# Fetching V rows apart from U rows, after GELU, in one of two gathers of a PEER trunk

## The chip, the cores and the metric

The kernel runs on one core of a Trainium2 chip. The metric is device time in microseconds, the median of several runs; one more execution is recorded by the hardware profiler. The engines are PE (TensorE, matmuls), PEld (its weight loads), DVE (VectorE), ACT (ScalarE), POOL (GpSimd, which issues the indirect DMAs), and SP (SyncE, which issues the plain DMAs). Sixteen DMA engines carry what both issue.

## The reference

A decoder trunk of four layers on 256 tokens of 1024 numbers. Each layer is a token mixer (HGRN2, FoX, Mamba-2 SSD, HGRN2) followed by a PEER feed-forward block. What the change touches is PEER:

```python
s = einsum('mhcd,hckd->mhck', q, sub_keys)         # 8 heads, 2 halves, 128 keys
sv, si = top_k(s, 16)                              # then the best 16 of 16 x 16 sums: idx, gates
u = take(u_tab, idx, axis=0)                       # (tokens, 8, 16, 1024) float32
v = take(v_tab, idx, axis=0)
act = gelu(einsum('md,mhkd->mhk', xb, u), approximate=False) * gates
return einsum('mhk,mhkd->md', act, v)
```

Each token picks 8 x 16 = 128 of a layer's 16384 experts and needs the U row and the V row of each, 4 KB apiece. `xb` is an RMS-normed token times `norm_ffn`; the inputs scale that weight by 7.294 (`factors = {'norm_ffn': 7.294, ...}`), and the rows of `peer_u` are independent normals of deviation 1/32. A V row whose GELU is 0 adds nothing to the sum.

## The kernel before

The work is cut into 8 stages (`STAGES`): layer l, token half t, 128 tokens each. A stage's expert sums run as 64 iterations, 8 heads times 8 pairs of experts (`pairs`, `NQ` = 8), while the mixer, the queries and the routing of the next stage run beside them in small steps.

An iteration i has two gathers, g = 0 and 1. Gather g brings, for 64 tokens and two experts each, 128 rows to 128 partitions (partition = 64 j + token). The table `uv` holds U and V of an expert side by side, so a row is 8 KB. There are eight buffers (`NGB` = 8, in `GB`, parts of the tile `arena`), each [128, 2048] float32: U in columns 0 to 1023, V behind it. Gather n = 2 i + g goes to buffer n % 8.

The order of work in each iteration is written out by hand (`ctx.enter_context(tc.manual_schedule())`); each engine runs its own instructions in that order, and waits are derived from which bytes an instruction reads and writes:

- `fetches(i)` (L1263, called at L1395) issues gathers on POOL's queue up to number 2 i + 7, which is pair i + 3, as far as `route` has their indices. A gather waits for the last reader of its buffer, the matmuls of `spread(i - 1)`.
- `dot(i, 0)` and `dot(i, 1)` (L1269): one DVE instruction each (`scalar_tensor_tensor`) multiplies U with the token rows `XR`, in place, and sums to `dots`.
- `spread(i)` (L1280): ACT takes GELU of both sums in one instruction, multiplies each by its gate, and scales a stack of two 64 x 64 identities to `dg`; PE then adds `dg` times V to the two banks `accs[s][e]`, e = 0 and 1 for the halves of V's columns, eight matmuls of 64 rows in all as the profile counts them (four in the source: two e, two g). The matmuls are at L1296.
- `route_steps` (three steps of the routing of a later head; DVE and some ACT), `others()` (the copies and vector work that follow the last step's matmuls) and `products_()` (the next step's matmuls).

`route` (L1164) ends by writing a head's indices as float32 and gates to `gs` and the int32 indices to `ix` (L1223).

Toward a stage's end: at i % 64 = 62 what is left of the side work is finished, and `repeated()` (L1241) turns the next stage's tokens on PE; at 63, ACT and DVE copy them to `XR` between and after the dots. At the first iteration of the next stage, between `dot(i, 0)` and `dot(i, 1)`, the first step of the side work adds the finished sums to the residual `h` (`normed`, called from `ready` with `accs.pop`, L1335): DVE waits there for the last matmul of the stage before. Weights come by SP's queue, 1 MB a unit (`loads`), three in flight beside those that have a place of their own.

Of the kernel before, what the change touches and what calls it, by code (L numbers as in the profile page):

```python
# [10 lines left out]
F32 = mybir.dt.float32  # L11
BF16 = mybir.dt.bfloat16
I32 = mybir.dt.int32
U32 = mybir.dt.uint32
U8 = mybir.dt.uint8
AF = mybir.ActivationFunctionType
OP = mybir.AluOpType
AX = mybir.AxisListType

P = 128  # L20
T = 256
D = 1024
DC = D // P
DEPTH = 4
# [4 lines left out]
NQ = TOPK // 2  # L29
NGB = 8  # L30
NRAW = 3
STAGES = 2 * DEPTH

KIND = ("hg", "fox", "ssd", "hg")
# [131 lines left out]
def trunk(ctx: ExitStack, tc: tile.TileContext, d: dict, out: bass.AP):  # L166
    nc = tc.nc
# [3 lines left out]
    wk2 = ctx.enter_context(tc.tile_pool(name="wk2", bufs=2))  # L171
# [22 lines left out]
    GB = [at_["gb"][:, i * 2 * D:(i + 1) * 2 * D] for i in range(NGB)]  # L194
# [12 lines left out]
    vec = Vector()  # L207
# [5 lines left out]
    def act(o, i, f, **k):  # L213

        if f not in ghosts:
            table[0] = f
        nc.scalar.activation(o, i, f, **k)  # L217
# [15 lines left out]
    m64 = cpool.tile([P, 64], F32, name="m64")  # L233
# [46 lines left out]
    def bank():  # L280
        return psp.tile([P, 512], F32, name="ps")
# [882 lines left out]
    def route(s, hh):  # L1164

        l = s // 2
        sv = wk2.tile([P, 2, TOPK], F32, name="sv")
        si = wk2.tile([P, 2, TOPK], U32, name="si", bufs=1)
        sf = wk2.tile([P, 2, TOPK], F32, name="sf", bufs=1)
        ts = wk2.tile([P, TOPK], F32, name="ts")  # L1170
        ti = wk2.tile([P, TOPK], U32, name="ti", bufs=1)
        ab = wk2.tile([P, 2, TOPK], U32, name="ab", bufs=1)
        af = wk2.tile([P, 2, TOPK], F32, name="af", bufs=1)
        cs = wk2.tile([P, TOPK * TOPK], F32, name="cs", bufs=1)
        eq = cs.bitcast(BF16).rearrange("p (c k j) -> p c k j", c=2, k=TOPK)
        cs = cs.rearrange("p (a b) -> p a b", a=TOPK)
        ix = wk2.tile([P, 2, NQ], I32, name="ix", bufs=4)
        gs = wk2.tile([P, 2, 2, NQ], F32, name="gs", bufs=4)
        gt = wk2.tile([P, 4], F32, name="gt")
        ig = wk2.tile([P, 2, TOPK], F32, name="ig")  # L1180
        yield from top16([(sv[:, c], si[:, c], SS[:, hh, c]) for c in range(2)])
        vec.tensor_copy(sf, si)
        tm(cs, sv[:, 0].unsqueeze(2).to_broadcast([P, TOPK, TOPK]),
           sv[:, 1][:, None, :].to_broadcast([P, TOPK, TOPK]), op=OP.add)
        yield
        yield from top16([(ts, ti, cs.rearrange("p a b -> p (a b)"))])
        vec.tensor_scalar(ab[:, 0], ti, 4, None, op0=OP.logical_shift_right)
        vec.tensor_scalar(ab[:, 1], ti, 15, None, op0=OP.bitwise_and)
        vec.tensor_copy(af, ab)
        m, z, r = (gt[:, i:i + 1] for i in range(3))  # L1190
        vec.tensor_scalar(m, ts[:, 0:1], -1.0, None, op0=OP.mult)
        act(ig[:, 1], ts, AF.Exp, bias=m, accum_out=z)
        yield
        eqv = eq.rearrange("p c k j -> p (c k) j")
        tm(eqv, C("iota")[:, None, :].to_broadcast([P, 2 * TOPK, TOPK]),
           af.rearrange("p c k -> p (c k)").unsqueeze(2).to_broadcast([P, 2 * TOPK, TOPK]), op=OP.is_equal)
        yield
        tm(eq, eq, sf.unsqueeze(2).to_broadcast([P, 2, TOPK, TOPK]), op=OP.mult)
        yield
        vec.tensor_reduce(af.rearrange("p c k -> p (c k)"), eqv, axis=AX.X, op=OP.add)  # L1200
        vec.tensor_scalar(sf[:, 0], af[:, 0], float(P), float(l * P * P), op0=OP.mult, op1=OP.add)
        tm(ig[:, 0], sf[:, 0], af[:, 1], op=OP.add)
        yield
        igv = ig.rearrange("p c (q j) -> p c q j", j=2)
        places = [(slice(j * 64, j * 64 + 64), g, slice(g * 64, g * 64 + 64), j) for j in range(2) for g in range(2)]

        def scaled():
            vec.reciprocal(r, z)
            vec.tensor_scalar(ig[:, 1], ig[:, 1], r, None, op0=OP.mult)

        if (s, hh) == (0, 0):

            for o, g, i, j in places:
                vec.tensor_copy(ix[o, g], igv[i, 0, :, j])
            scaled()
            for o, g, i, j in places:
                vec.tensor_copy(gs[o, g, 1], igv[i, 1, :, j])
        else:
            scaled()
            yield  # L1220
            for o, g, i, j in places:
                vec.tensor_copy(gs[o, g], igv[i, :, :, j])
            vec.tensor_copy(ix, gs[:, :, 0])  # L1223
        got[s, hh] = ix, gs

    heads = [(s, hh) for s in range(STAGES) for hh in range(8)]
# [28 lines left out]
    accs = {}  # L1255
    sent = [0]

    def fetch(n):
        (s, hh, q), g = pairs[n // 2], n % 2
        nc.gpsimd.indirect_dma_start(GB[n % NGB], None, d["uv"],  # L1260
                                     bass.IndirectOffsetOnAxis(ap=got[s, hh][0][:, g, q:q + 1], axis=0))

    def fetches(n):  # L1263

        while sent[0] < 2 * len(pairs) and sent[0] < 2 * n + NGB and pairs[sent[0] // 2][:2] in got:
            fetch(sent[0])
            sent[0] += 1

    def dot(i, g):  # L1269
        if g == 0:  # L1270
            acts[i] = wk2.tile([P, 3, 2], F32, name="dots", bufs=4)
        u = GB[(2 * i + g) % NGB][:, 0:D]
        stt(u, u, 1.0, XR[:, g], op0=OP.mult, op1=OP.mult, accum_out=acts[i][:, 0, g:g + 1])

    def warm(n, b, x):

        for _ in range(n):
            nc.tensor.matmul(b, x[:, 0:P], x[:, 0:512], start=True, stop=True)

    def spread(i):  # L1280
        s, hh, q = pairs[i]
        a = acts.pop(i)
        dg = wk2.tile([P, 2, 64], F32, name="dg", bufs=4)
        act(a[:, 1], a[:, 0], AF.Gelu)
        for g in range(2):
            act(a[:, 2, g:g + 1], a[:, 1, g:g + 1], AF.Copy, scale=got[s, hh][1][:, g, 1, q:q + 1])
        for g in range(2):
            act(dg[:, g], m64, AF.Copy, scale=a[:, 2, g:g + 1])
        if hh == 0 and q == 0:
            accs[s] = [accp.tile([P, 512], F32, name="acc") for _ in range(2)]  # L1290
        if i == len(pairs) - 1:
            warm(3, bank(), cst)
        for e in range(2):
            for g in range(2):
                v = GB[(2 * i + g) % NGB][:, D + e * 512:D + (e + 1) * 512]
                nc.tensor.matmul(accs[s][e][g * 64:g * 64 + 64], dg[:, g], v, start=hh == 0 and q == 0,  # L1296
                                 stop=hh == 7 and q == NQ - 1)


    mixers = {"hg": hgrn, "fox": fox, "ssd": ssd}  # L1300
# [67 lines left out]

    for s in range(STAGES):
        work = side(s) if s else chain(first, side(0))  # L1370
        state = {"open": False, "done": False, "pe": 0.0, "dve": 0.0, "cost": 0.0, "slot": 0}

        def products_(force=False):

            state["slot"] += 1
            if state["done"] or not (force or state["cost"] < SIDE[s] * state["slot"] / SPAN):
                return
            state["pe"], state["dve"] = pe[0], dve[0]
            r = next(work, work)
            state["done"] = r is work  # L1380
            state["open"] = r is None
            state["pe"] = pe[0] - state["pe"]
            state["dve"] = dve[0] - state["dve"]

        def others():

            if state["open"]:
                d0 = dve[0]
                next(work)
                state["open"] = False  # L1390
                state["cost"] += max(state["pe"] / 4.6, (state["dve"] + dve[0] - d0) / 2.2, 0.5)

        for i in range(64 * s, 64 * s + 64):
            new, end = i % 64 == 0 and s > 0, i % 64 == 63 and s + 1 < STAGES
            fetches(i)  # L1395
            dot(i, 0)
            if end:
                for o, b in x[:2]:
                    nc.scalar.copy(o, b)
            elif new:  # L1400

                products_(True)
                others()
            dot(i, 1)
            spread(i)
            if end:
                (_, b), (o, c) = x[2:]
                nc.scalar.copy(x[2][0], b)
                vec.tensor_copy(o, c)
            route_steps(3, i // 8 + 3)  # L1410
            others()
            products_()
            if i % 64 == 62 and s + 1 < STAGES:
                while not state["done"]:
                    others()
                    products_(True)
                others()
                x = repeated()
            if table[0] is not AF.Gelu:
                act(spare, eps, AF.Gelu)  # L1420
        others()
        for _ in work:
            pass
# [17 lines left out]
```

## Time and profile before

| | |
|---|---|
| median of three runs | 3184.8 us (3184.7 to 3185.98) |
| profiled execution, its own time | 3185.7 us |
| its span, first to last instruction | 3183.9 us |
| mean granted TensorE clock | 0.904 |
| first and last gather issued at | 117.2 and 3157.7 us |
| gathers, of them waited for by DVE | 1024, 540 |
| read from HBM | 1299.92 MB |

How to read it: the span is cut by the gathers. Up to about 120 us the kernel computes the first mixer and the first indices; then 512 iterations run, some 5.9 us each ((3157.7 - 117.2) / 512), and after the last gather there are 26 us to the end of the span. A stretch's row of the busy-time view has its bounds and length, the busy us of PE, PEld, DVE, ACT and POOL with their instruction counts, then the granted clock, the DMA engines' busy share and GB/s. In a row of a group of instructions the numbers behind the count are busy us and mean ns of one, then the idle time just before them and what ended it. In a row of waits they are us in total, times, and the longest.

### The profile page before, as it was taken

The page shows a single profiled execution, that of the slowest core. Times are in us where ns is not written, and L with a number is a line of the kernel's source. Part 1 is how long each engine was busy: PE and PEld are TensorE (multiplying, and loading weights), DVE is VectorE, ACT ScalarE, POOL GpSimd, SP SyncE. Part 2 cuts the span into 40 slices and gives each one's busy share as a digit, 9 for nine tenths or more (in the row PEclk, how much of TensorE's full clock was granted, in tenths as well). Part 3 has the DMA queues.
Part 4 walks back from the last instruction along what each step waited for, and adds up shares of the span by engine and source line. Part 5 has one row for each costly group of instructions (what it writes and reads, how often), then busy time and mean ns, then how long its engine had stood idle before and what let it go on. Part 6 is the DMA issues. An engine that isn't in the chain of part 4 may idle for free.

```text
span 3183.9 us, 30834 instructions
## 1 busy us (share of the span) xinstructions
PE 2470.2 (78%) x8610; PEld 1095.2 (34%) x8610; DVE 2115.5 (66%) x5584; ACT 1351.3 (42%) x3895; POOL 1189.5 (37%) x1032
## 2 busy tenths in 40 slices
PE   9888787877787876889878898778876877865655
PEld 4433333332333423344333443333332333332222
DVE  2576657675676756878567786476666767676764
ACT  3354324353344523577334773244433543333332
POOL 0243334343343424433334333244433433344443
PEclk9999898988899988999989998989988999898787
DMA  7899999999999999999999999999999999999997
GB/s 299 339 420 421 421 421 419 421 407 421 407 420 421 407 422 414 404 421 421 417 417 401 421 419 415 416 403 410 421 421 421 401 421 421 421 414 421 415 417 330
DMA packets 180025, 1303.02 MB, mean 409 GB/s; under 512 B 19984, under 2 KB 20368, under 8 KB 21520
## 3 DMA queue, kind: packets, MB, share of 16 engines
q0 software_dynamic: 147456, 1073.81, 81.8%
q1 hardware_dynamic: 32400, 227.24, 17.3%
q8 instruction: 72, 1.18, 0.2%
q14 instruction: 97, 0.79, 0.1%
HBM read 1299.92 MB, written 1.05 MB: 409 GB/s over the span
## 4 chain that ended last, share of the span: by engine, by line
DMA 58%; PE 14%; DVE 11%; issue 9%; ACT 4%; POOL 3%; POOLq 0%; DVEq 0%; ACTq 0%
DMA arena<-in_uv,ix 58%; DVE arena L204 8%; PE acc L1296 7%; PE pj L239 5%; POOL arena L1260 3%; PE ps L239 2%; ACT dots L217 1%; ACT L217 1%; DVE cs L204 1%; ACT dg L217 1%; PE ps L243 0%; DVE si L204 0%; ACT arena L217 0%; DVE sv L204 0%; DVE af L204 0%
## 5 line engine op out<-in xcount | busy, mean ns | idle before, releaser
L1260 POOL DMA_INDIRECT arena<-in_uv,ix x1024 | 1185.4, 1158 | 1968.6 <-PE acc L1296 1411.0
L204 DVE SCALAR_TENSOR_TENSOR arena<-arena 128x1024 f32<-128x1024 f32 (+3 forms) x1282 | 1322.1, 1048 | 878.5 <-DMA arena<-in_uv,ix 834.9
L1296 PE MATMUL acc<-arena,dg 128*64 128x512 f32 x4096 | 1285.2, 714 | 693.9 <-ACT dg L217 693.2
L1296 PEld LDWEIGHTS acc<-arena,dg 128*64 128x64 f32 x4096 | 466.0, 152 | 1326.4 <-ACT dg L217 1004.2
L217 ACT ACTIVATE dots<-dots 128x2 f32<-128x2 f32 x512 | 103.2, 202 | 1549.4 <-DVE arena L204 1549.3
L239 PE MATMUL pj<-raw,arena 128*128 128x512 f32 (+1 forms) x1368 | 635.5, 607 | 3.8 <-DMA raw<-in_ssm 2.8
L217 ACT ACT_TABLE_LOAD x325 | 417.0, 1283 | 6.8 <-DVE arena L204 0.8
L239 PEld LDWEIGHTS pj<-raw,arena 128*128 128x128 f32 x1368 | 249.8, 193 | 393.6 <-issue 377.4
L217 ACT ACTIVATE dg<-m,dots 128x64 f32<-128x64 f32 x1024 | 292.5, 333 | 0.0
L239 PE MATMUL pj<-arena 128*128 128x512 f32 x568 | 267.4, 616 | 0.3 <-DVE arena L204 0.3
L217 ACT ACTIVATE dots<-dots,gs 128x1 f32<-128x1 f32 x1024 | 245.6, 287 | 16.7
L239 PEld LDWEIGHTS pj<-arena 128*128 128x128 f32 x568 | 106.4, 197 | 162.5 <-issue 153.2
L239 PE MATMUL ps<-arena 128*128 128x128 f32 (+3 forms) x992 | 129.5, 286 | 1.1 <-ACT arena L1125 0.9
L239 PEld LDWEIGHTS ps<-arena 128*128 128x128 f32 (+2 forms) x992 | 102.7, 167 | 65.3 <-issue 39.0
L243 PEld LDWEIGHTS ps<-fst,arena 128*128 128x128 f32 x568 | 67.3, 147 | 85.5 <-issue 39.9
L243 PE MATMUL ps<-fst,arena 128*128 128x128 f32 x568 | 90.9, 288 | 4.5 <-ACT arena L1124 2.5
L217 ACT ACTIVATE arena<-arena 128x512 f32<-128x512 f32 (+3 forms) x132 | 67.7, 555 | 42.0 <-DVE arena L204 39.5
L204 DVE DVE_READ_ACCUMULATOR arena<-arena 128x1 f32 x1024 | 85.0, 83 | 0.0
L204 DVE FIND_INDEX8 si<-sv,arena 128x8 uint32<-128x128 f32 x256 | 69.9, 286 | 0.0
L239 PE MATMUL ps<-cst,arena 128*128 128x128 f32 (+3 forms) x288 | 67.0, 360 | 0.0
L204 DVE MAX8 sv<-arena 128x8 f32<-128x128 f32 x256 | 61.8, 283 | 5.7 <-ACT arena L1129 5.7
L217 ACT ACTIVATE arena<-ps 128x512 f32<-128x512 f32 (+3 forms) x114 | 43.7, 425 | 29.7 <-PE ps L239 29.0
(116 smaller groups left out, 1248.9 us busy)
## 6 DMA issues: line engine op xcount, KB each, us to landing
raw<-in_hg SPq DMA_DIRECT2D x57, 1024.0 KB, 9.4
raw<-in_ssm SPq DMA_DIRECT2D x56, 1024.0 KB, 9.4
raw<-in_wq SPq DMA_DIRECT2D x32, 1024.0 KB, 9.2
raw<-in_fox SPq DMA_DIRECT2D x24, 1024.0 KB, 9.2
arena<-in_wq SPq DMA_DIRECT2D x17, 1024.0 KB, 16.7
arena<-in_uv,ix POOLq DMA_INDIRECT x1024, 14.9
arena<-in_hg SPq DMA_DIRECT2D x15, 1024.0 KB, 14.1
arena<-in_keys SPq DMA_DIRECT2D x4, 1024.0 KB, 9.3
```

What stands on the lines that cost most here:

```text
L204: return getattr(nc.vector, name)(o, *a, **k)
L217: nc.scalar.activation(o, i, f, **k)
L239: nc.tensor.matmul(o, w, m, start=start, stop=stop)
L243: nc.tensor.transpose(o, i, ident)
L1260: nc.gpsimd.indirect_dma_start(GB[n % NGB], None, d["uv"], bass.IndirectOffsetOnAxis(ap=got[s, hh][0][:, g, q:q + 1], axis=0))
L1296: nc.tensor.matmul(accs[s][e][g * 64:g * 64 + 64], dg[:, g], v, start=hh == 0 and q == 0, stop=hh == 7 and q == NQ - 1)
```

## The change

From the ninth iteration on, gather 0 brings its U rows only (from a view `parts` of the table with twice as many rows of half the length, at row 2 x index), into columns 0 to 1023. Its V rows come by a DMA of their own, `second(i)`, issued after `dot(i, 1)` into columns 1024 to 2047, at row 2 x index + 1. Where the GELU of gather 0 is equal to 0, a large number is added to the index, so that it lies beyond the table, and the DMA is told to leave such rows out; the buffer keeps what it held, and that is multiplied by 0. For the last two iterations of a stage (`early`) V is fetched without regard to GELU, one iteration ahead of the dots. GELU is taken for each gather apart, right after its dot. The matmuls of gather 0 move to `spread(i + 2)` (`LAG` = 2), ahead of those of (i + 2, 1); at the end of a stage those of its last two iterations are done in their own iteration as well. Gather 1 is as it was.

```diff
+LAG = 2
+WHOLE = 8
+FAR = 1048576.0
...
             vec.tensor_copy(ix, gs[:, :, 0])
+            vec.tensor_scalar(ix[:, 0], gs[:, 0, 0], 2.0, None, op0=OP.mult)
+            vec.tensor_scalar(gs[:, 0, 0], gs[:, 0, 0], 2.0, 1.0, op0=OP.mult, op1=OP.add)
...
+    parts = d["uv"].rearrange("r (k n) -> (r k) n", k=2)
+
+    def early(i):
+        return i % 64 >= 64 - LAG
+
     def fetch(n):
-        (s, hh, q), g = pairs[n // 2], n % 2
-        nc.gpsimd.indirect_dma_start(GB[n % NGB], None, d["uv"],
+        i, g = divmod(n, 2)
+        s, hh, q = pairs[i]
+        to, src = GB[n % NGB], d["uv"]
+        if not g and i >= WHOLE:
+            to, src = to[:, 0:D], parts
+        nc.gpsimd.indirect_dma_start(to, None, src,
                                      bass.IndirectOffsetOnAxis(ap=got[s, hh][0][:, g, q:q + 1], axis=0))
...
+    def second(i):
+
+        if i < WHOLE or i >= len(pairs):
+            return
+        s, hh, q = pairs[i]
+        iv = wk2.tile([P, 1], I32, name="iv", bufs=4)
+        row = got[s, hh][1][:, 0, 0, q:q + 1]
+        to = GB[2 * i % NGB][:, D:2 * D]
+        if early(i):
+            nc.vector.tensor_copy(iv, row)
+            nc.gpsimd.indirect_dma_start(to, None, parts, bass.IndirectOffsetOnAxis(ap=iv, axis=0))
+        else:
+            far = wk2.tile([P, 1], F32, name="far", bufs=2)
+            nc.vector.tensor_scalar(far, acts[i][:, 1, 0:1], 0.0, FAR, op0=OP.is_equal, op1=OP.mult)
+            nc.vector.tensor_tensor(iv, far, row, op=OP.add)
+            nc.gpsimd.indirect_dma_start(to, None, parts, bass.IndirectOffsetOnAxis(ap=iv, axis=0),
+                                         bounds_check=2 * DEPTH * P * P - 1, oob_is_err=False)
 
     def dot(i, g):
...
+        act(acts[i][:, 1, g:g + 1], acts[i][:, 0, g:g + 1], AF.Gelu)
...
+    diags = {}
 
     def spread(i):
...
-        act(a[:, 1], a[:, 0], AF.Gelu)
...
-            act(dg[:, g], m64, AF.Copy, scale=a[:, 2, g:g + 1])
+            diags[i, g] = wk2.tile([P, 64], F32, name="dg%d" % g, bufs=4 - g)
+            act(diags[i, g], m64, AF.Copy, scale=a[:, 2, g:g + 1])
...
+        sums = [(i, 1)]
+        if i < WHOLE or early(i):
+            sums.append((i, 0))
+        if (i - LAG, 0) in diags:
+            sums.insert(0, (i - LAG, 0))
         for e in range(2):
-            for g in range(2):
-                v = GB[(2 * i + g) % NGB][:, D + e * 512:D + (e + 1) * 512]
-                nc.tensor.matmul(accs[s][e][g * 64:g * 64 + 64], dg[:, g], v, start=hh == 0 and q == 0,
-                                 stop=hh == 7 and q == NQ - 1)
+            for j, g in sums:
+                v = GB[(2 * j + g) % NGB][:, D + e * 512:D + (e + 1) * 512]
+                nc.tensor.matmul(accs[s][e][g * 64:g * 64 + 64], diags[j, g], v, start=j % 64 == 0,
+                                 stop=j % 64 == 63)
...
             fetches(i)
+            if early(i + 1):
+                second(i + 1)
             dot(i, 0)
...
             dot(i, 1)
+            if not early(i):
+                second(i)
             spread(i)
```

More of the change, by code (lines that the diff above doesn't have):

```diff
@@ L1282, in spread @@
         a = acts.pop(i)
-        dg = wk2.tile([P, 2, 64], F32, name="dg", bufs=4)
-        act(a[:, 1], a[:, 0], AF.Gelu)
         for g in range(2):
@@ L1292, in spread @@
             warm(3, bank(), cst)
-        for e in range(2):
-            for g in range(2):
-                v = GB[(2 * i + g) % NGB][:, D + e * 512:D + (e + 1) * 512]
-                nc.tensor.matmul(accs[s][e][g * 64:g * 64 + 64], dg[:, g], v, start=hh == 0 and q == 0,
-                                 stop=hh == 7 and q == NQ - 1)
+        sums = [(i, 1)]
[3 more added lines that the diff above has]
+            sums.insert(0, (i - LAG, 0))
+        for e in range(2):
+            for j, g in sums:
+                v = GB[(2 * j + g) % NGB][:, D + e * 512:D + (e + 1) * 512]
+                nc.tensor.matmul(accs[s][e][g * 64:g * 64 + 64], diags[j, g], v, start=j % 64 == 0,
+                                 stop=j % 64 == 63)
+        for k in sums:
+            diags.pop(k)
     mixers = {"hg": hgrn, "fox": fox, "ssd": ssd}
```

## The prediction

> **What bounds the kernel now.** I read the page's head, slices and queues first, then the chain that ended last, then the waits, and last the busy time by stretches.
>
> ```profile
> span 3183.9 us, 30834 instructions
> ...
> PE 2470.2 (78%) x8610; PEld 1095.2 (34%) x8610; DVE 2115.5 (66%) x5584; ACT 1351.3 (42%) x3895; POOL 1189.5 (37%) x1032
> ...
> GB/s 299 339 420 421 421 421 419 421 407 421 407 420 421 407 422 414 404 421 421 417 417 401 421 419 415 416 403 410 421 421 421 401 421 421 421 414 421 415 417 330
> DMA packets 180025, 1303.02 MB, mean 409 GB/s; under 512 B 19984, under 2 KB 20368, under 8 KB 21520
> ...
> q0 software_dynamic: 147456, 1073.81, 81.8%
> q1 hardware_dynamic: 32400, 227.24, 17.3%
> ...
> DMA 58%; PE 14%; DVE 11%; issue 9%; ACT 4%; POOL 3%; POOLq 0%; DVEq 0%; ACTq 0%
> ...
> L1260 POOL DMA_INDIRECT arena<-in_uv,ix x1024 | 1185.4, 1158 | 1968.6 <-PE acc L1296 1411.0
> ...
> L217 ACT ACTIVATE dots<-dots 128x2 f32<-128x2 f32 x512 | 103.2, 202 | 1549.4 <-DVE arena L204 1549.3
> ...
> arena<-in_uv,ix POOLq DMA_INDIRECT x1024, 14.9
> ```
> ```profile
> POOL arena L1260 <- PE acc L1296: 1411.0, 428, 10.5
> ...
> DVE arena L204 <- DMA arena<-in_uv,ix: 834.9, 540, 5.4
> ```
> ```profile
> 300.00:360.00 60.00, 50.18 (x175) 21.34 (x173) 41.06 (x99) 23.42 (x64) 21.44 (x20) 0.91 1.01 421
> ...
> 1600.00:2000.00 400.00, 336.27 (x1227) 153.92 (x1228) 295.33 (x807) 207.23 (x548) 144.39 (x126) 0.93 1.01 415
> ...
> 3100.00:3184.00 84.00, 47.93 (x126) 17.99 (x126) 40.09 (x68) 21.25 (x83) 26.96 (x23) 0.78 0.81 335
> ```
>
> The last two numbers of a stretch are the DMA engines' busy share and GB/s. From the third slice to the last but one the rate is 401 to 422, and the share is 1.01 even where PE is busiest (336 of 400 us): the 16 DMA engines are full. DVE waits 835 us for gathers, and POOL 1411 us for a buffer that PE must free; these waits are symptoms of the full queue. The two gathers of an iteration carry 82% of the bytes. So a byte not moved is worth its time at 421 GB/s, a packet added costs time, and work on an engine is free until it lets the DMA ring run dry.
>
> **The bytes.** Of 512 iterations, the first 8 (WHOLE) stay as they were and 504 are split. Sixteen of those (two a stage, `early`) bring their V rows unconditionally; 488 bring V after GELU and leave rows out: 128 x 4096 B = 0.524 MB each, 255.9 MB in all. How many GELUs are exactly 0 no trace shows. The dot product of a normed token (its weights scaled by 7.294) with a row of independent normals of variance 1/1024 is normal with deviation 7.294. GELU is x times the normal distribution function. If zero starts where 1+erf rounds away in float32, at -5.4, 23.0% of rows go; if where the product itself leaves float32's normal range, near -13, 3.7%. I take the middle, 13.3%: 34.0 MB, at 421 GB/s **-81 us** (ends -23 and -140). A row out of bounds is taken to cost nothing; the other case is a rival.
>
> **The packets.** 147456 packets are 144 per gather: on each of 16 engines 8 rows and 1 that signals. A split iteration has U (9), the whole gather (9) and V (9), where it had 18: 504 x 9 = 4536 more per engine, less the 488 x 8 x 0.133 = 519 skipped, 4017. What a packet costs beside its bytes I bound by the start of the trace, where two loads of shorter rows run between loads of 8 KB rows.
>
> ```profile
> cst<-in_const SPq DMA_DIRECT2D x1, 584.5 KB, 11.5
> ...
> par<-in_par SPq DMA_DIRECT2D x1, 416.0 KB, 12.0
> ```
> ```profile
> 0.00:5.00 5.00, 3.51 (x4) 1.51 (x5) 0.54 (x2) 2.08 (x4) 1.16 (x5) 1.00 0.63 215
> 5.00:10.00 5.00, 4.48 (x15) 2.00 (x14) 2.50 (x6) 2.32 (x6) 0.00 (x0) 1.00 1.01 411
> 10.00:15.00 5.00, 5.00 (x13) 2.15 (x12) 0.42 (x2) 0.00 (x0) 0.00 (x0) 1.00 1.02 419
> 15.00:20.00 5.00, 5.00 (x13) 2.28 (x12) 0.14 (x2) 0.60 (x1) 0.00 (x0) 1.00 1.00 422
> 20.00:25.00 5.00, 5.00 (x13) 2.20 (x12) 0.00 (x0) 2.46 (x3) 0.00 (x0) 1.00 1.01 423
> ```
> ```profile
> 10.00:12.00 2.00, 2.00 (x6) 0.82 (x5) 0.00 (x0) 0.00 (x0) 0.00 (x0) 1.00 0.97 405
> 12.00:14.00 2.00, 2.00 (x6) 0.95 (x5) 0.00 (x0) 0.00 (x0) 0.00 (x0) 1.00 1.05 427
> ...
> 34.00:36.00 2.00, 2.00 (x9) 0.99 (x8) 0.00 (x0) 0.00 (x0) 0.00 (x0) 1.00 0.93 240
> ```
>
> By the rates, 3.1 MB have moved at 10 us and 5.2 at 15; x, first and three weight units ahead are 3.77 MB, so both loads (1.02 MB, rows of 4.6 and 3.3 KB) lie between 10 and 15 us. In 8 KB rows they would be 141 packets; they are 288, or 9.2 more per engine. 419 against 422.5 GB/s is 0.041 us lost in 5 us: 4.5 ns a packet, say 5. Finer windows give the ends: 0 (427 at 12 to 14 us) and, if all the shortfall of 10 to 12 us were theirs, 0.083 us, 9 ns. The 240 GB/s at 34 to 36 us (0.86 us) belongs to `gn`, one 512-byte row read 128 times; a gather reads different rows, so I exclude it. 4017 x 5 ns = **+20 us** (0 to 36).
>
> [...]
>
> **The new waits.** POOL now issues, in iteration i, U of pair i+3, the whole gather W of i+3, then V of i. W waits for `spread(i-1)`, which now waits for V(i-3). V(i) waits for GELU(i) and two DVE instructions; behind it in POOL's queue stand U and W of i+4, which DVE and PE wait for. When V(i-3) lands, the ring still holds U, W, V twice and one U: 2 x 2.03 + 0.52 = 4.6 MB, 10.9 us. Against that stand `spread`'s eight matmuls, two POOL issues of 1.16 us, and the way from issue to the first bytes, at most the shortest issue to landing of any gather (5.8 us) less its own 1.05 MB (2.5 us):
>
> ```profile
> 507.06 2.17 PE L1296 MATMUL acc<-arena,dg 128*64 128x512 f32 x8 [1.51 <-ACT dg L217]
> ```
> ```profile
> L1260 POOL DMA_INDIRECT arena<-in_uv,ix x1024: 932/942/2872, 117.2 to 3157.7; - x171
> ...
> DMA to landing us min/median/max: 5.8/14.9/32.5
> ```
>
> 2.2 + 2.3 + 3.3 = 7.8 us: it fits with 3.1 us to spare. Today the ring holds three pairs, 6.3 MB or 14.9 us, as the median says. I put the steady state at **0**; if the cover goes, the lateness is lost once per three iterations. Behind a late V on PE stand the other sums, the side work's matmuls and, on DVE and ACT, whoever evacuates these; they move later together.
>
> **Stage ends** are thinner. V62 and V63 go into the ring behind U64, W64 and U65, W65, and the stage's sum is complete only with them, while today it needs pair 63 alone.
>
> ```profile
> 512.76 0.69 DVE L204 COPY arena<-ps 128x512 f32<-128x512 f32 x1 [1.77 <-PE ps L239]
> 513.37 1.21 DVE L204 SCALAR_TENSOR_TENSOR arena<-arena 128x1024 f32<-128x1024 f32 x1
> 514.51 0.08 DVE L204 DVE_READ_ACCUMULATOR arena<-arena 128x1 f32 x1
> 514.51 1.28 DVE L204 TENSOR_TENSOR arena<-acc,arena 128x512 f32<-128x512 f32 x2
> 515.71 1.22 DVE L204 SCALAR_TENSOR_TENSOR arena<-arena 128x1024 f32<-128x1024 f32 x1
> ```
>
> Those 1.28 us are the residual adds between the two dots of pair 64. They will wait for V63, and dot(64,1), V64 and W68 stand behind them. When V63 lands the ring holds U66, W66, U67: 2.1 MB, 5 us. W67 needs 2.2 us of matmuls, 1.2 of POOL and 3.3 to its first bytes, 6.7; V64 needs 2.2 of matmuls, 0.7 for the second add, 1.3 for the dot, 0.3 for DVE's two new instructions, and then the same 1.2 and 3.3, 9.0, when W67 ends at 9.2. So the ring is empty for about 2 us, and the margin stays near nothing until DVE has caught up two iterations. Ends: 0 and 8 us (all 5 us of ring lost and DVE's 3 us of backlog). I take 4, for seven stage ends **+28 us** (0 to 56).
>
> **Hidden work.**
>
> ```profile
> 1002.80 0.15 DVE L204 TENSOR_SCALAR gt<-ts 128x1 f32<-128x1 f32 x1
> ```
>
> DVE: two such a split iteration and two small ones a head, about 170 us, in the 835 us in which it waits for gathers. ACT: one GELU more an iteration at 0.2 us, 103 us, in 1549 us of waiting; DVE's first new instruction waits for the GELU, which starts late in only 512 - 425 cases. POOL: 504 issues at 1.16 us, 584 us, in 1969 idle (at the slowest issue seen, 2.87, 1446). Uncovered, these three would cost 170, 103 and 584. PE does the same matmuls.
>
> **The tail.**
>
> ```profile
> 3170.47 1.23 DVE L204 SCALAR_TENSOR_TENSOR arena<-arena 128x1024 f32<-128x1024 f32 x1 [1.06 <-DMA arena<-in_uv,ix]
> ...
> 3173.88 1.94 PE L1296 MATMUL acc<-arena,dg 128*64 128x512 f32 x8
> ```
>
> The last bytes are now V511, whose dot and GELU are long done: **-3 us**.
>
> **Sum:** -81 + 20 + 28 - 3 = -36 on the profiled execution's 3185.7 us (its span plus 1.8), which lies 0.9 above the median of the runs: 3149 us. Its own ends are -84 (packets and stage ends free), 3101, and +6, 3191 (both at their upper ends).
>
> **Rivals.**
>
> 1. A packet costs the 9 ns of the upper end: -81 + 36 + 28 - 3 = -20, 3165. For it: 405 GB/s as the short rows begin at 10 us; against: 427 in the next two. [...]
> 2. Skipped rows aren't free: each moves as before or takes its slot. Then -0 + 23 + 28 - 3 = +48, 3233, slower. Nothing in this trace shows a skipped row; for it speaks only that the queue's packet count has been fixed at 144 so far.
> 3. Zero starts lower, near -13: -23 + 22 + 28 - 3 = +24, 3209, slower.
> 4. Zero starts at -5.4: -140 + 18 + 28 - 3 = -97, 3088.
> 5. The loop V(i-3), `spread(i-1)`, W(i+3), V(i) becomes the bound where PE is fullest. It decides once PE is over 3.1 us late when V lands. If it is an iteration late there, 6 us, 2.9 us are lost per three iterations; over two stages, 128 iterations, 124 us: 3273, slower. For it: 84% busy PE takes V's wait in order. Against: its lateness moves with DMA, which is full today at that load.
> 6. Packets and stage ends near their upper ends eat the gain: -81 + 30 + 50 - 3 = -4, 3181, no change.
>
> **Chances.** Forecast 0.42; rival 1 0.20, 2 0.10, 3 0.07, 4 0.05, 5 0.08, 6 0.08. Faster by over 0.2% (6 us, about what a measurement of this kernel can tell from no change) are the forecast, 1 and 4: 0.67; within it 6: 0.08; slower 2, 3 and 5: 0.25. The range 3101 to 3233 runs from the forecast's lower end to rival 2 and leaves out 4 and 5, 0.13; the likeliest case's own range, without the part of its ends that rivals 1 and 6 hold, is 3101 to 3165.
>
> **What would show it.** Queue 0's MB: 1073.8 less 34 if the share is right, unchanged if rows aren't skipped; its packets about 147456 + 504 x 144 less one per skipped row. GB/s in full stretches: some 417 at 5 ns, below 414 at 10. DMA share below 1.01 in the middle of stages would show rival 5; dips near the seven changes of stage the 28 us. PE should now wait for DMA ahead of the acc matmuls, and POOL for DVE. I am wrong if the DMA share falls everywhere, or if POOL's issue with a bounds check takes several us.

## The result

| | before | after |
|---|---|---|
| median us | 3185.39 (3184.7 to 3186.49, 4 runs) | 3210.73 (3204.24 to 3213.19, 4 runs) |
| profiled execution, its own time | 3185.7 | 3209.99 |
| its span | 3183.9 | 3208.2 |

The ratio of the times is 1.0076, with a 95% interval of 1.0059 to 1.0094. The change makes the kernel 25 us slower; the forecast was 3149 us, 36 us faster.

### The profile page after: what moved, and what is told of

Same layout as the page of the kernel before. It is cut to its first block, busy times and chain, and to the rows that moved or that the text cites. A ratio compares the mean times of both kernels' runs of the same rounds, so it can differ in the third digit from the quotient of the medians.

```text
span 3208.2 us, 33399 instructions
## 1 busy us (share of the span) xinstructions
PE 2506.6 (78%) x8610; PEld 989.7 (31%) x8610; DVE 2232.1 (70%) x6702; ACT 1383.7 (43%) x4407; POOL 1799.3 (56%) x1536
## 2 busy tenths in 40 slices
DMA packets 252623, 1271.08 MB, mean 396 GB/s; under 512 B 35902, under 2 KB 36286, under 8 KB 158608
## 3 DMA queue, kind: packets, MB, share of 16 engines
q0 software_dynamic: 220032, 1041.70, 81.2%
HBM read 1299.92 MB, written 1.05 MB: 406 GB/s over the span
## 4 chain that ended last, share of the span: by engine, by line
DMA 37%; issue 15%; DVE 14%; PE 12%; POOL 11%; ACT 5%; POOLq 0%; DVEq 0%; ACTq 0%
DMA arena<-in_uv,iv 26%; DMA arena<-in_uv,ix 10%; DVE arena L207 8%; POOL arena L1274 8%; PE acc L1335 6%; PE pj L242 4%; POOL arena L1298 3%; ACT L220 2%; PE ps L242 2%; DVE cs L207 1%; ACT arena L220 1%; DVE gs L207 1%; DVE iv L1297 1%; DVE af L207 1%; DVE si L207 1%
## 5 line engine op out<-in xcount | busy, mean ns | idle before, releaser
L1335 PE MATMUL acc<-arena,dg 128*64 128x512 f32 x4096 | 1318.9, 720 | 675.6 <-DMA arena<-in_uv,iv 597.5
L1274 POOL DMA_INDIRECT arena<-in_uv,ix x1024 | 1212.6, 1184 | 1067.5 <-PE acc L1335 640.0
L207 DVE SCALAR_TENSOR_TENSOR arena<-arena 128x1024 f32<-128x1024 f32 (+3 forms) x1282 | 1299.0, 1045 | 382.0 <-DMA arena<-in_uv,ix 380.3
L1335 PEld LDWEIGHTS acc<-arena,dg 128*64 128x64 f32 x4096 | 364.5, 154 | 1441.0 <-DMA arena<-in_uv,iv 861.0
L1298 POOL DMA_INDIRECT arena<-in_uv,iv x488 | 563.4, 1155 | 311.5 <-DVE iv L1297 93.3
L220 ACT ACTIVATE dots<-dots 128x1 f32<-128x1 f32 x1024 | 190.4, 199 | 1165.5 <-DVE arena L207 1164.6
L242 PE MATMUL pj<-raw,arena 128*128 128x512 f32 (+1 forms) x1368 | 642.4, 613 | 1.0 <-ACT arena L657 0.7
L1296 DVE TENSOR_SCALAR far<-dots 128x1 f32<-128x1 f32 x488 | 72.9, 149 | 221.2 <-ACT dots L220 221.1
L1297 DVE TENSOR_TENSOR iv<-far,gs 128x1 int32<-128x1 f32 x488 | 77.7, 159 | 16.8
L1115 ACT COPY arena<-ps 128x512 f32<-128x512 f32 x31 | 18.1, 583 | 134.1 <-PE ps L242 134.1
## 6 DMA issues: line engine op xcount, KB each, us to landing
arena<-in_uv,ix POOLq DMA_INDIRECT x1024, 10.3
```

Source lines behind the costliest of these rows:

```text
L207: return getattr(nc.vector, name)(o, *a, **k)
L242: nc.tensor.matmul(o, w, m, start=start, stop=stop)
L1115: nc.scalar.copy(SS[:, 2 * g:2 * g + 2], b.rearrange("p (h c k) -> p h c k", h=2, c=2))
L1274: nc.gpsimd.indirect_dma_start(to, None, src, bass.IndirectOffsetOnAxis(ap=got[s, hh][0][:, g, q:q + 1], axis=0))
L1296: nc.vector.tensor_scalar(far, acts[i][:, 1, 0:1], 0.0, FAR, op0=OP.is_equal, op1=OP.mult)
L1297: nc.vector.tensor_tensor(iv, far, row, op=OP.add)
```

## The profile after

The page of the kernel after (head, slices, queues, chain, groups, landing times):

```profile
span 3208.2 us, 33399 instructions
...
PE 2506.6 (78%) x8610; PEld 989.7 (31%) x8610; DVE 2232.1 (70%) x6702; ACT 1383.7 (43%) x4407; POOL 1799.3 (56%) x1536
...
GB/s 295 342 411 415 409 402 377 415 412 416 409 368 416 400 413 385 394 416 405 417 405 355 408 415 404 408 361 413 415 415 402 365 416 416 412 370 402 408 413 329
DMA packets 252623, 1271.08 MB, mean 396 GB/s; under 512 B 35902, under 2 KB 36286, under 8 KB 158608
...
q0 software_dynamic: 220032, 1041.70, 81.2%
...
DMA 37%; issue 15%; DVE 14%; PE 12%; POOL 11%; ACT 5%; POOLq 0%; DVEq 0%; ACTq 0%
...
L1274 POOL DMA_INDIRECT arena<-in_uv,ix x1024 | 1212.6, 1184 | 1067.5 <-PE acc L1335 640.0
...
L1298 POOL DMA_INDIRECT arena<-in_uv,iv x488 | 563.4, 1155 | 311.5 <-DVE iv L1297 93.3
...
arena<-in_uv,ix POOLq DMA_INDIRECT x1024, 10.3
```

The bytes did go: q0 carries 1041.70 MB instead of 1073.81. Two things stand against it. The full slices are at 415 to 417 GB/s where they were at 421: that is the price of more and shorter packets, as e2_split below shows. And there are now dips, to 377, 368, 385, 355, 361, 365 and 370, some five slices (400 us) apart: the seven changes of stage. The chain that ended last is no longer mainly DMA (58% before, 37% now); "issue", DVE and POOL have taken its place. A gather lands 10.3 us after its issue in the median instead of 14.9, so less is queued ahead of the DMA engines to live on.

Stretches of the kernel after: bounds and length, busy us of PE, PEld, DVE, ACT and POOL, then clock, DMA share and GB/s.

```profile
300.00:360.00 60.00, 49.05 (x173) 19.25 (x171) 42.98 (x119) 23.74 (x76) 33.64 (x28) 0.89 1.02 414
504.00:552.00 48.00, 34.63 (x158) 13.89 (x156) 32.96 (x96) 18.28 (x62) 27.14 (x25) 0.83 0.92 352
512.00:516.00 4.00, 4.00 (x27) 1.88 (x25) 0.00 (x0) 0.00 (x0) 1.00 (x2) 0.76 0.92 369
516.00:520.00 4.00, 4.00 (x58) 3.34 (x54) 1.19 (x2) 2.59 (x8) 0.87 (x1) 1.00 0.94 325
520.00:524.00 4.00, 2.19 (x8) 0.43 (x4) 3.02 (x7) 0.20 (x1) 0.94 (x1) 1.00 0.46 129
524.00:528.00 4.00, 1.93 (x4) 0.47 (x4) 3.97 (x19) 1.25 (x6) 2.81 (x3) 1.00 0.92 335
528.00:532.00 4.00, 1.93 (x6) 0.48 (x6) 3.93 (x17) 2.48 (x10) 3.11 (x3) 1.00 0.80 263
532.00:536.00 4.00, 2.49 (x6) 0.47 (x6) 3.90 (x14) 3.87 (x8) 3.10 (x3) 0.80 0.91 305
536.00:540.00 4.00, 2.56 (x6) 0.98 (x8) 3.49 (x15) 3.95 (x12) 2.97 (x3) 0.50 1.01 414
...
1800.00:1900.00 100.00, 93.84 (x390) 45.28 (x388) 83.19 (x250) 74.72 (x188) 52.35 (x44) 1.00 1.01 409
```

The same stretch around the stage end in the kernel before:

```profile
504.00:552.00 48.00, 36.60 (x179) 18.77 (x176) 35.97 (x91) 19.66 (x63) 22.89 (x20) 0.88 1.01 417
```

Inside a stage the DMA engines are as full as before: the share is 1.02 at 300 to 360 us, and 1.01 at 1800 to 1900 us, where PE is busy for 94 of 100 us. Around the first change of stage (504 to 552) the share is 0.92 against 1.01; it falls to 0.46 and is whole again 24 us after the first short stretch. What happens there, in the timeline of the kernel after (start, us, instruction, idle time before it and what ended it):

```profile
511.05 3.78 PE L1335 MATMUL acc<-arena,dg 128*64 128x512 f32 x7 [3.01 <-DMA arena<-in_uv,iv]
...
514.69 0.94 POOL L1274 DMA_INDIRECT arena<-in_uv,ix  x1 [5.32 <-PE acc L1335]
515.10 3.66 PE L242 MATMUL ps<-fst,arena 128*64 128x128 f32 x62
...
515.93 0.94 POOL L1274 DMA_INDIRECT arena<-in_uv,ix  x1 [0.30 <-issue]
...
518.59 3.60 PE L1335 MATMUL acc<-arena,dg 128*64 128x512 f32 x12
...
518.81 0.69 DVE L207 COPY arena<-ps 128x512 f32<-128x512 f32 x1 [12.72 <-PE ps L242]
...
521.64 0.94 POOL L1274 DMA_INDIRECT arena<-in_uv,ix  x1 [4.77 <-PE acc L1335]
522.22 0.69 DVE L207 TENSOR_TENSOR arena<-acc,arena 128x512 f32<-128x512 f32 x1 [0.98 <-PE acc L1335]
```

PE waits until 511.05 for V62. In its queue, the products of V62, the matmuls that turn the next stage's tokens (64 in all, 62 of them in the row shown) and the products of iteration 63 with V63 all stand behind that wait. DVE needs the turned tokens for dot(64,0): it stands still for 12.72 us, where it stood for 1.77 before. POOL waits 5.32 and 4.77 us for buffers that these products hold, and meanwhile the DMA engines run dry: their share goes from 0.92 at 512 to 516 us to 0.46 at 520 to 524.

**Where the time went.** The trace records every DMA packet with its size and duration. In the kernel after, a row of 8 KB takes 312 ns in the median, one of 4 KB 160, the short signal at the end of a DMA 9; and a row left out is still there, as a packet of 4 bytes that also takes 9 ns. Packets times these durations over 16 engines is the time that full queues would need ("packets" below). What the span has beyond it is called idle time of the queues here. It holds real gaps and also packets that took longer than the median, as they do where the queues run thin (at 520 to 524 us a share of 0.46 moves 129 GB/s, where 1.02 moves 414). The packet records themselves add up to 3165.2 us before and 3165.9 after, so much of "idle" is slow packets and not gaps. It is cut at the starts of dots: "head" to the first dot, "ends" from dot 60 of a stage to dot 14 of the next (seven of them), "tail" from dot 60 of the last stage, "middle" the rest.

```
us               span  packets  idle   head  middle  ends  tail
before         3183.7   3113.2  70.4   33.6     6.5  13.4  17.1
after          3207.9   3076.3 131.6   34.5    17.2  63.6  16.4
e1_noskip      3275.5   3150.4 125.2   36.5    12.6  60.0  16.1
e2_split       3215.1   3150.2  64.9   34.4     2.4  11.3  17.0
e3_vahead      3170.2   3076.3  93.9   33.3    17.9  26.5  16.3
e4_adds        3203.2   3076.3 126.9   36.7    20.3  54.2  15.8
e5_tokens      3194.0   3076.3 117.7   34.4    22.9  44.1  16.5
e6_all         3157.1   3076.2  80.9   34.8    19.7  12.2  14.2
e7_nolast      3162.0   3076.2  85.8   34.4    25.4  11.9  14.2
e8_both        3296.4   3038.3 258.1   33.8   117.7  93.3  13.3
e9_own         3147.5   3076.2  71.3   34.7    13.3   9.3  14.1
e10_nogelu     3221.5   3150.2  71.3   34.8    17.8   5.7  13.0
```

(Spans here are counted from the first working instruction, 0.2 to 0.4 us less than on the pages.) Between before and after: packets -37, ends +50, middle +11, head +1, tail -1, together +24. Each row is one execution, and a few us in "middle" say little: the seven kernels with the packets of the kernel after have 13 to 25 there, though most differ only at the stage ends. The gain in bytes is there; the ends of the stages alone take more than is left of it.

## The experiments

Two theories. **The first**: the change does what it says, but pays for it at the stage ends and in packets. **Rival**: leaving rows out brings little or nothing (a skipped row is not free), and the order of the work around the late V is the loss. The runs named e1 and e2 take the packets apart, e3, e4, e5 and e7 the stage ends, e6 puts the repairs together, e8 doubles the change, and e9 and e10 ask for the middle. Ratios are to runs of the kernel before that were taken beside each experiment (medians 3183.45 to 3184.1).

### e1_noskip: the kernel after, but every V row comes

```diff
-FAR = 1048576.0
+FAR = 0.0
```

> The changed kernel with every V row fetched (the number added for a zero GELU is 0), all waits and the order kept. If a skipped row saves its bytes and pays one small packet, as the changed kernel's queue says (32.1 MB and 7854 short packets), this costs 32.1 MB / 415 GB/s - 7854 x 9 ns / 16 = 77 - 4 = +73 us: about 3283. If the V rows come late anyway and the bytes left out are lost again as idle time, it stays within 20 us of 3211.

Measured 3275.61 us, ratio 1.0283 (1.0268 to 1.0298): 2.07% of 3184.1, 66 us, above the kernel after. The page of e1_noskip:

```profile
DMA packets 252622, 1303.20 MB, mean 398 GB/s; under 512 B 28048, under 2 KB 28432, under 8 KB 158608
...
q0 software_dynamic: 220032, 1073.84, 81.7%
```

The packet count of q0 is 220032 in both kernels: a row left out does not leave the queue. But 28048 packets under 512 B become 35902 with rows left out, 7854 more, which is 12.57% of 488 x 128. Each is 151 ns shorter than a row of 4 KB: 7854 x 151 / 16 = 74 us of packets, and 66 us in the time, since e1_noskip's fuller queues are idle for 6 us less. The rival falls: skipping works, for 9 ns a row.

### e2_split: the kernel before, gather 0 cut in two halves

```diff
+        if not g and n // 2 >= WHOLE:
+            for k, at in enumerate((got[s, hh][0][:, 0, q:q + 1], vrow[s, hh][:, q:q + 1])):
+                nc.gpsimd.indirect_dma_start(GB[n % NGB][:, k * D:(k + 1) * D], None, parts,
+                                             bass.IndirectOffsetOnAxis(ap=at, axis=0))
+            return
```

> The kernel before with gather 0 cut in two halves, U rows and V rows, issued one behind the other; no lag, no skipping, no wait on GELU. It has the packets of the change alone: 504 x 9 more per engine. At my 5 ns a packet +23: 3208; if a half row takes 4 ns more than half of a row's 312 ns and the signal 9 ns, 504 x (16 x 4 + 9) = 37: 3222. If the changed kernel's loss were the packets' (the rival of packets at over 9 ns), +100 or more: above 3285.

Measured 3219.16 us, ratio 1.0109 (1.0095 to 1.0124), a cost of 35 us (30 to 39). The products, the GELU and the buffers are as before; besides the packets only 504 more issues on POOL and two small DVE instructions a head are new. By the packet durations a halved row costs 2 x 160 - 312 = 8 ns more, and 504 iterations have 8 such rows and one signal more on each engine: 504 x (8 x 8 + 9) = 36.8 us. The two agree. The page of e2_split:

```profile
GB/s 296 350 416 416 416 417 406 416 415 417 413 414 416 400 415 413 399 417 413 415 398 408 417 416 412 414 391 410 416 417 416 397 416 417 410 415 415 410 411 327
...
q0 software_dynamic: 220032, 1073.84, 82.5%
```

The full slices stand at 416 to 417, as in the kernel after, and there are no dips at the stage changes. So the rate comes from the packets, and the dips come from the late V.

### e3_vahead: the last two V's ahead of the later gathers

```diff
-            fetches(i)
             if early(i + 1):
                 second(i + 1)
+            fetches(i)
             dot(i, 0)
```

> The changed kernel with the V rows of a stage's last two pairs issued ahead of the gathers of the same iteration, so that V63 lands ahead of U65 and W65 (1.57 MB, 3.7 us). Theory: each stage end costs some 11 us because its sum is complete only when V63 has landed. Then 7 x 3.5 = 25 us less: 3186, and DVE's 12.7 us wait at the first stage end some 4 us shorter. If the loss comes from slower packets everywhere or from the added DVE work, no change: 3211.

Measured 3174.2 us, ratio 0.9971 (0.996 to 0.9982): 12 us further than expected, and 1.05% (33 us) below the kernel after. The stretches of e3_vahead at the first stage end:

```profile
512.00:516.00 4.00, 4.00 (x54) 3.14 (x51) 1.41 (x2) 2.56 (x8) 0.65 (x1) 1.00 1.02 421
516.00:520.00 4.00, 1.97 (x6) 0.41 (x3) 2.98 (x8) 0.33 (x3) 0.94 (x1) 1.00 0.91 328
520.00:524.00 4.00, 1.93 (x4) 0.47 (x4) 3.97 (x18) 1.27 (x8) 3.02 (x3) 1.00 0.90 346
524.00:528.00 4.00, 1.93 (x6) 0.48 (x6) 3.93 (x15) 2.45 (x12) 3.09 (x4) 1.00 0.86 288
```

The stretch at 0.46 is gone; idle time at the seven ends falls from 63.6 to 26.5 us by moving, twice a stage, one DMA of 0.5 MB past two others (U and W, 1.6 MB together). DVE's wait at the first end is 9.31 us instead of 12.72, nearly the 4 us less that were expected. Order in POOL's queue was most of the cost.

### e5_tokens and e4_adds: which of DVE's two waits is it?

At the stage end DVE needs two things of PE: the turned tokens (for dot(64,0)) and the finished sums (for the residual adds). e5_tokens holds back the products of iteration 62 until the tokens are turned:

```diff
-            spread(i)
+            held = i % 64 == 62 and s + 1 < STAGES
+            if not held:
+                spread(i)
...
                 x = repeated()
+                spread(i)
```

> The changed kernel with the last side work of a stage and the turning of the next tokens issued on PE ahead of the sums of pair 62, so that they don't stand behind V62. If V63 alone holds the stage end, the adds still wait for it: 0 to 2 us less each, 3197 to 3211. If the hold is the turning of the tokens behind V62 (dot 64 can't start), 5 to 8 us less each: 3155 to 3176.

Measured 3195.34 us, ratio 1.0035 (1.0023 to 1.0048), 0.41% (13 us) below the kernel after: a little below what the wait for V63 alone predicted and far from the 3155 to 3176 of the other theory. The timeline of e5_tokens:

```profile
506.84 0.69 DVE L207 COPY arena<-ps 128x512 f32<-128x512 f32 x1 [1.85 <-PE ps L242]
507.45 1.22 DVE L207 SCALAR_TENSOR_TENSOR arena<-arena 128x1024 f32<-128x1024 f32 x1
...
517.83 0.69 DVE L207 TENSOR_TENSOR arena<-acc,arena 128x512 f32<-128x512 f32 x1 [9.16 <-PE acc L1335]
```

DVE now waits for the tokens no longer than in the kernel before (1.85 us), dot(64,0) starts 12 us earlier than in the kernel after, and then DVE waits 9.16 us for the sums. A wait was taken away and the next one came to stand behind it.

e4_adds leaves the tokens as they are and moves the adds behind dot(64,1) and V64:

```diff
-            elif new:
-
-                products_(True)
-                others()
             dot(i, 1)
             if not early(i):
                 second(i)
+            if new:
+                products_(True)
+                others()
             spread(i)
```

> The changed kernel with the residual adds of a new stage moved behind dot(64,1) and the issue of V64, so that these don't stand behind V63 on DVE. Theory of the stage end: the ring gets V64 about 5 us sooner and DVE has one dot less to catch up: 2 to 4 us less at each of seven, 3183 to 3197. If only the landing of V63 counts, nothing: 3211.

Measured 3202.04 us, ratio 1.0054 (1.0041 to 1.0068), 0.22% (7 us) below the kernel after, less than the 14 to 28 expected: alone it frees little, since DVE has waited for the tokens first. Neither of the two waits is the cause by itself; both end when the last V rows have come and their products are done, which e7_nolast puts to the test.

### e7_nolast: the kernel after without that wait

The products of gather 0 of a stage's last two iterations, (62,0) and (63,0), are left out of the sums; their rows are still fetched.

```diff
-        if i < WHOLE or early(i):
+        if i < WHOLE:
             sums.append((i, 0))
...
-                                 stop=j % 64 == 63)
+                                 stop=j % 64 == 63 or g == 0 and j % 64 == 61)
```

> The changed kernel without the products of gather 0 of a stage's last two pairs (left out of the sums; their rows are still fetched). The adds then wait for V61 instead of V63, 2.1 MB or 5 us earlier in the ring: by the theory of the stage end 7 x 5 = 35 us less, 3176. If the ends cost what they cost for another reason (DVE's backlog, the last side work), no change: 3211.

Measured 3161.54 us, ratio 0.9921 (0.9906 to 0.9936), 49 us below the kernel after and 14 further than expected. The bytes and packets are the same; idle time at the ends is 11.9 us, as in the kernel before. The timeline of e7_nolast:

```profile
511.29 0.69 DVE L207 COPY arena<-ps 128x512 f32<-128x512 f32 x1 [7.41 <-PE ps L242]
511.90 1.22 DVE L207 SCALAR_TENSOR_TENSOR arena<-arena 128x1024 f32<-128x1024 f32 x1
513.04 1.28 DVE L207 TENSOR_TENSOR arena<-acc,arena 128x512 f32<-128x512 f32 x2
```

Two stretches of e7_nolast right behind that:

```profile
512.00:516.00 4.00, 1.06 (x6) 0.18 (x2) 3.97 (x10) 0.71 (x5) 0.94 (x2) 1.00 1.02 417
516.00:520.00 4.00, 1.93 (x4) 0.47 (x4) 3.97 (x17) 1.28 (x8) 3.39 (x3) 1.00 1.02 416
```

DVE still waits 7.41 us for the tokens, since PE waits for an ordinary V ahead of them, and that costs nearly nothing: the DMA share is 1.02 from 512 to 520 us and then 0.94 and 0.97 for 4 us each. In the kernel after, where the wait was 12.72 us, it fell to 0.46. The adds do not wait at all. So the wait for V62 and V63, with the few products that are left out too, is the whole of the stage-end loss, 63.6 - 11.9 = 52 us, 7 us for each of seven ends.

### e6_all: the repairs together

e3_vahead, e4_adds and e5_tokens in one kernel, six buffers for `iv` instead of four, and the idle matmuls `warm()` (L1311) one iteration earlier. In the tail of the kernel after these had come to stand ahead of the last products:

```profile
3188.97 5.60 PE L1335 MATMUL acc<-arena,dg 128*64 128x512 f32 x12 [2.02 <-DMA arena<-in_uv,iv]
...
3194.50 2.84 PE L1311 MATMUL ps<-cst 128*128 128x512 f32 x6
...
3197.27 3.65 PE L1335 MATMUL acc<-arena,dg 128*64 128x512 f32 x12
```

```diff
-        iv = wk2.tile([P, 1], I32, name="iv", bufs=4)
+        iv = wk2.tile([P, 1], I32, name="iv", bufs=6)
...
-        if i == len(pairs) - 1:
+        if i == len(pairs) - 2:
             warm(3, bank(), cst)
```

> The changed kernel with the three edits of the stage end together (V ahead of the gathers, tokens ahead of the sums of pair 62, adds behind V64), two more index buffers for V, and the three idle matmuls of the tail one iteration earlier. By the packets' own time the lost time at the stage ends is 63.6 us against 13.4 before. If the edits remove the wait on V, ends come to about 15 and the tail gains 3: 3211 - 49 - 3 = 3159. If they only shift it, it stays at the 3174 of the first edit alone.

Measured 3158.34 us (3154.75 to 3163.91), ratio 0.992 (0.9906 to 0.9933): 0.8% faster than the kernel before and some 1.6% faster than the kernel after, with nothing left out. The page of e6_all:

```profile
span 3157.3 us, 32958 instructions
...
GB/s 295 345 404 416 410 405 414 414 415 408 408 409 414 396 416 405 409 416 405 417 402 386 403 414 403 406 398 411 415 412 407 404 416 415 415 407 405 408 415 338
...
q0 software_dynamic: 220032, 1041.70, 82.0%
```

The same packets as in the kernel after, and no dip below 386. Against the kernel before: packets -37, ends -1, middle +13, tail -3, head +1.

### e8_both: e6_all with gather 1 split and skipped too

V of both gathers comes late, `second(i, g)` for g = 0 and 1, the products of both move to `spread(i + 2)`, and the small buffers are shared out anew (an extract):

```diff
-        if not g and i >= WHOLE:
+        if i >= WHOLE:
...
-            diags[i, g] = wk2.tile([P, 64], F32, name="dg%d" % g, bufs=4 - g)
+            diags[i, g] = wk2.tile([P, 64], F32, name="dg%d" % g, bufs=3 + g)
...
-                second(i)
+                second(i, 0)
+                second(i, 1)
```

> The kernel of the three edits with gather 1 split and skipped as well. Packets at their median times: +37 for the halves, -74 for the rows left out: 37 us less than e6_all if the DMA ring stays full, 3122. If POOL's four issues an iteration (4.8 us of 5.6) or DVE's two more instructions become the bound, it is no faster than e6_all, and the DMA share in the middle of stages falls below 1.

Measured 3311.23 us, ratio 1.0416 (1.0395 to 1.0438), slower. Packets need another 38 us less, but the queues stand idle for 258 us. A stretch that runs into the last stage (which begins at 2908 us and has little side work beside it), and a line of the waits of e8_both:

```profile
2800.00:3100.00 300.00, 214.12 (x591) 62.93 (x590) 218.01 (x711) 95.34 (x365) 237.43 (x206) 0.84 0.94 343
```
```profile
ACT dg L220 <- PE acc L1335: 559.1, 227, 7.7
```

In that stretch POOL is busy for 237.43 us with 206 issues, and 0.30 us lie between two of them (as ahead of the issue at 515.93 us in the kernel after): 237.4 + 206 x 0.30 = 299 of 300 us. With four issues an iteration POOL has become the bound there. In the earlier stages there is a second possible cause that this run doesn't part from it: with three buffers for gather 0's `dg`, ACT waits 559 us for PE. So e8_both shows a bound for this stretch and is inconclusive for the rest.

### e9_own and e10_nogelu: the middle of the stages

Some 11 us of the loss lie between the ends. Two theories: the late V holds the buffer of the whole gather, since its products stand ahead of the iteration's own ("loop"), or V is issued late because it waits for GELU ("late issue"). e9_own is e6_all with the own products first:

```diff
-            sums.insert(0, (i - LAG, 0))
+            sums.insert(1, (i - LAG, 0))
-        for e in range(2):
-            for j, g in sums:
+        for j, g in sums:
+            for e in range(2):
```

> e6_all with one thing more: in spread(i) the products of (i,1) come first and those of (i-2,0) behind them, so that the gather W(i+3) no longer waits for V(i-2) or V(i-3) through the products in front of its own. Of e6_all's span of 3157.1 us 80.9 us are not filled by packets, 19.7 of them in the middle of the stages; the kernel before has 6.5 there. Theory 'loop' (the middle is lost because a late V holds W's buffer): the middle comes down to 5 to 10 and the time to 3143 to 3149. Theory 'late issue' (it is lost because V is issued only once GELU is known, behind DVE and ACT, so that POOL stands still with U and W behind V): the order of the products changes nothing there, 3155 to 3162.

e10_nogelu is e6_all with V issued at the same place, but without regard to GELU, and all rows:

```diff
-        if early(i):
+        if True:
             nc.vector.tensor_copy(iv, row)
```

> e6_all, but V is issued at the same place without regard to GELU and every V row comes: it does not wait for GELU, and nothing is skipped. The bytes and packets are those of e1_noskip and e2_split (3150 us by their packets' durations), head and tail as in e6_all (about 49), ends 12. Theory 'late issue': the middle goes back to that of e2_split, 2.4, so 3214 plus 2: 3213 to 3218. Theory 'loop': the middle stays near that of e1_noskip, 12.6, or higher, so 3223 to 3230.

e9_own: 3157.54 us (3149.55 to 3161.11), ratio 0.9918 (0.9902 to 0.9935), the same as e6_all, although the wait that it aimed at did become shorter. The waits of e6_all, and of e9_own:

```profile
POOL arena L1274 <- PE acc L1335: 600.4, 323, 8.0
...
DVE far L1296 <- ACT dots L220: 214.9, 126, 6.0
```
```profile
POOL arena L1274 <- PE acc L1335: 364.3, 229, 7.0
...
DVE far L1296 <- ACT dots L220: 199.7, 122, 5.7
```

POOL waits 236 us less for PE and nothing comes of it in the median. The profiled execution, 3149.55, is the fastest of four that reach to 3161.11, so the 6 us by which its middle is shorter can't be laid to the edit. The mean granted clock, though, is 0.949 to 0.951 in all four, where e6_all has 0.893 to 0.904 and e10_nogelu, taken beside it, 0.888 to 0.895. So it goes with the edit, and the time did not follow it. e10_nogelu: 3222.34 us (3220.5 to 3224.03), ratio 1.0117 (1.01 to 1.0134), with 17.8 us idle in the middle though V waits for no GELU. So e9_own speaks against the loop as the only cause (its middle, 13.3, lies between what the two theories say), e10_nogelu against the late issue, and each alone would have spoken for the other. The middle is lost in single places rather than steadily: in the first stage of the kernel after, 4.1 us around iterations 4 to 8 (3.7 there in the kernel before, too), 1.0 at 44 to 48 and 2.6 at 52 to 56, and nothing between. e2_split, with the same packets but V right behind U, has 2.4 us in all the middles. What e2_split lacks and all the others have is V's later place in the queue and its products two iterations later; which of the waits that come with these carries the 11 us stays open.

## Why the prediction was wrong

The sum on record was -81 (bytes) + 20 (packets) + 28 (stage ends) + 0 (steady state) - 3 (tail) = -36. Measured, in the same order: **-74 + 37 + 50 + 11 - 1**, and +1 in the head, = +24. The byte, packet, stage-end and tail terms are there in the trace, mis-sized; the steady state, put at nothing, was not nothing. The errors all go in one direction: 7, 17, 22, 11, 2 and 1. The measured 3211 lies in the range 3101 to 3233 only because that reached up to rival 2, of which next to nothing happened; that is luck. The sum's upper end, given as +6, is +8 by its own terms (-81 + 36 + 56 - 3).

- **Bytes**: -81 forecast, -74 measured. 12.57% of the late rows are left out, not 13.3%; so, if the sums are spread as the prediction took, GELU is zero below about -8.4 (the point under which 12.57% of a normal of deviation 7.294 lie). Neither of the two origins considered, -5.4 and -13, is there: that the middle of their shares came close was luck. A row left out saves 151 of 160 ns, not all.
- **Packets**: the first step that failed, short by 17 us. The count was too small by 519, since a skipped row stays a packet, but the price was the larger part: "4.5 ns a packet, say 5" against (8 x 8 + 9) / 9 = 8.1 ns measured. It had been read from the difference of two rounded rates, 419 and 422.5 GB/s, over 5 us. The window of 12 to 14 us, read as "no cost" at 427 GB/s, holds by the packet records almost nothing but the short rows, so it can't be read to a few GB/s. The records, which the trace of the kernel before has too, show that the same loads cost as much as the gathers: 131 ns for 3.3 KB and 181 for 4.6 KB both fit 8 ns plus 0.0371 ns a byte, as do 160 for 4 KB and 312 for 8 KB. The finer window's 9 ns, taken as the upper end, was the better reading.
- **Stage ends**: the step that decided, short by 22 us. Its mechanism was named (the sums complete only with V63, the adds wait, gathers stand behind) and e7_nolast shows that it is all of the loss. Forecast were 4 us an end, measured are 7, near the upper bound of 8. What the working left out is PE's queue: it let dot(64,0) run on time and began DVE's wait at the adds. In fact the matmuls that turn the tokens stand behind V62's products on PE, so dot(64,0) itself waits, 12.72 us. DVE then has a backlog of the whole wait and not of 3 us, and the stretches stay below full until 536 us. e5_tokens is the kernel that the working had in mind, with the tokens in time and DVE's wait at the adds: its ends cost 44.1 - 13.4 = 31 us more than before, close to the 28. So PE's queue is what the term lacked.
- **Steady state**: 0 forecast, +11 measured, by single places, of unknown cause. In the full stretches it holds, with a share of 1.01 to 1.02, and the 10.9 us estimated for what is queued ahead of V are near the median landing of 10.3.
- **Hidden work**: right as far as the full stretches show. DVE has 117 us more, ACT 32 and POOL 610 (170, 103 and 584 were forecast), and the DMA engines stay full beside it, at a share of 1.01 to 1.02. e8_both shows where it ends for POOL: at four issues an iteration.
- **Tail**: -3 forecast, -1 measured. The idle matmuls of `warm()` came to stand between the products of the last V rows; in e6_all, where they are moved, it is -3.

Of the rivals, **6** (packets and stage ends near their upper ends) is nearest to what happened; it allowed 30 and 50 for them and still counted -81 for the bytes and nothing for the middle, so it came to 3181. **1** had the packets right at 36: e2_split measures 35 and the packet records 37, where 20 was chosen. **3** gives almost the measured time, 3209, for a reason that is not there: it leaves out 9.5 MB, and in fact 32.1 MB were left out; **4** would leave out 58.9. **2** is refuted by e1_noskip (66 us slower when all rows come) but for its 9 ns a row, and **5** by the share of 1.01 where PE is fullest (1800 to 1900 us).

Of the signs named beforehand, q0's MB, the rates of 415 to 417, the dips at the stage changes and the waits of PE for DMA and of POOL for DVE came as written; that q0's packet count would fall by one for every skipped row did not.

## What to carry to other kernels

Where DMA is full, work out the price of more packets from single packet durations, and not from rates that are rounded over a few microseconds: here half of the gain in bytes went there. When a transfer is made later, go to the places where something must be complete (the end of a stage, the last sum) and follow every in-order queue through them, the engine that does unrelated work behind the late product included; the steady state told nothing of it. A late transfer that the end needs goes ahead of those that are only prefetched: that one line was worth 33 us here.

## What the runs showed of the hardware

- A row that an indirect DMA leaves out for its index stays in the queue as a packet of 4 bytes with 9 ns, and POOL's issue takes 62 ns longer with the limit than without (medians of 999 ns, L1298, and 937, L1293).
- By the median durations of the records (131, 160, 181 and 312 ns) a packet costs 8 ns beside its bytes at 3.3, 4, 4.6 and 8 KB alike; the 35 us of e2_split agree.
- The "HBM read" of the page of the profile, 1299.92 MB before and after, does not fall with rows left out; the queue's own MB do.
- A wait of 7.4 us on DVE at the stage end cost nearly nothing (e7_nolast), one of 9.3 us cost 2 us an end (e3_vahead) and one of 12.7 us cost 7 (after), where a gather lands 10.3 us after its issue in the median. That fits a cost of what a wait outlasts the queue by, and of the backlog after it; no run varied the wait alone.
